# Down product of a seven-product feed-forward layer: the last gated pair stays on the chip and is used third, the residual is added in the middle visits, weights are loaded through GpSimd's queue

## The chip, the cores and the metric

The kernel runs on one core of a Trainium2 chip. The metric is the device time of one launch in microseconds (us). The engines are called by the profile's names: PE is TensorE (PEld its weight loads), DVE is VectorE, ACT is ScalarE, POOL is GpSimd, SP is SyncE, whose queue issues most DMAs. A "q" behind a name (SPq, POOLq) is that engine's sequencer, which works off its instructions strictly in order.

## The reference, cut to what matters

Two layers; each ends with a feed-forward block. Model width is 1024, there are 1024 tokens, and the hidden width is 2816.

```python
def swiglu(h, w_gate, w_up, w_down):
    return (jax.nn.silu(h @ w_gate) * (h @ w_up)) @ w_down

for layer in range(2):
    x = x + mixer(rms_norm(x, ...))
    x = x + memory_cross_attention(rms_norm(x, ...), m, ...)
    x = x + swiglu(rms_norm(x, g_ffn[layer]), w_gate[layer], w_up[layer], w_down[layer])
```

Everything is float32. The change touches only the last product of `swiglu`, and the addition to x.

## The kernel before, in words

Activations lie transposed: 128 features on the partitions, 1024 tokens along the free axis. A *pair* is two such chunks of 128 features, so a 256 x 1024 block, taken as 2 x 2 sub-blocks of 128 x 512. Every block product is formed from seven products of sums of sub-blocks instead of eight (`seven`, L1815). Each operand is cut into a high and a low half that PE multiplies in its rounded float32 format, so one product is three matmuls of 128x512 (`mm`, L441). Making an operand is one ACT copy (high) and one DVE subtraction (low, L454), beside the sums.

Two arenas in on-chip memory hold all data: R (35 x 1024 columns, operands that PE reads) and F (16 x 1024 columns, plain float32; its part "a" is the first 8 x 1024, part "b" the other 8 x 1024). A planner in Python (`run`, L468) walks a list of tasks, one task for each of the seven products, allots space, and makes operands `la` columns ahead of their first use; `raws` bounds how many weight blocks are loaded ahead, `f_reserve` is the part of F that such loads must leave free. The framework's scheduler then orders each engine's instructions by the planner's priorities; each engine and each DMA queue runs its list in order.

The feed-forward block (`ffn`, L1894) runs in two stages. *Gate and up*: for j = 0 to 10, a unit of `w_gate` and one of `w_up` (256 columns, `Unit`, L202) are multiplied with the four pairs of the input, `gated` applies silu, `upped` multiplies the two. `store` (L1926) turns the resulting pair j into its seven operands with four POOL subtractions (L1933), seven ACT copies (L1937) and seven DVE subtractions (L454, through `low`), each in a slot of R, and writes them to device memory `pq` through SP's queue (L1941, seven DMAs for a pair). *Down*: 14 visits (`VISITS`, L32) each take one pair of output chunks (mp = 0 to 3), a stretch lo to hi of the eleven stored pairs, and the block of `w_down` that belongs to them; each of the four output pairs is visited three or four times. The stored pairs come back through SP's queue (`Stored.make`, L361, two DMAs for each operand, 14 for a pair), the weights too (L223). Results are added from PE's accumulator onto x by DVE (`onto_x`, L1876, L1883). `x_back` (L2044, L2047) loads x, which already holds everything but this block's result, into part "a" before the visits: two chunks at j = 9, six at the start of down.

In the first visits everything comes together: the operands of pairs 0 and 1 are loaded into slots of R that the last up unit (j = 10) gives back, pair 10 is still being split and stored, and the weights of the first visits come in.

## Time and profile before

| | |
|---|---|
| median of 3 runs | 2439.45 us (2435.73 to 2440.53) |
| the profiled execution's own time | 2443.61 us |
| its span, first to last instruction | 2441.5 us |
| PE busy | 2356.0 us (96%) |
| DVE busy | 1714.9 us (70%) |
| ACT busy | 1008.5 us (41%) |
| POOL busy | 712.3 us (29%) |
| mean granted TensorE clock | 0.986 of full speed |
| DMA | 350.25 MB, 143 GB/s over the span |

The down stage of layer 0 runs from about 1114 to 1320 us of the span, that of layer 1 from about 2200 to 2430 us. Busy PE is 96% of the span, so what can be won is the rest, and what a lower clock takes from the busy time. It is read stage by stage: a table by windows shows where PE is not busy, the timeline of each engine shows what it waits for there.

### The profile page before, as it was taken

How to read it: one execution, taken by the hardware profiler on the slowest of the kernel's cores; microseconds unless marked ns; L12 is line 12 of the kernel's file. 1: busy time of each engine (PE TensorE's matmuls, PEld its weight loads, DVE VectorE, ACT ScalarE, POOL GpSimd, SP SyncE). 2: the span in 40 equal slices, each digit the busy share in tenths (PEclk: the TensorE clock that was granted, in tenths of full speed). 3: DMA queues.
4: the chain of work that ended last, by engine and by line, in shares of the span. 5: the costliest groups of instructions: out<-in, count | busy, mean ns of one | idle time of the engine just before them, and what ended most of it. 6: DMA issues, size and time to landing. Idle time of an engine off the chain costs nothing.

```text
span 2441.5 us, 31142 instructions
## 1 busy us (share of the span) xinstructions
PE 2356.0 (96%) x11358; PEld 1984.2 (81%) x11358; DVE 1714.9 (70%) x2521; ACT 1008.5 (41%) x1826; POOL 712.3 (29%) x707
## 2 busy tenths in 40 slices
PE   7999999999999999997999999999999999998999
PEld 7999889888878778776888788888878888876887
DVE  5456467864888788878667653355888989887765
ACT  5345366745444444443223311145544444443221
POOL 6542233343433333331001310043433334331000
PEclk9999999999999999999999999999999999999999
DMA  7336334430224344449863221021224434459773
GB/s 229 117 132 208 96 99 136 128 115 27 95 89 153 121 154 150 172 168 340 275 215 117 61 78 52 26 66 48 104 73 143 157 136 165 158 173 382 238 246 95
DMA packets 251649, 350.25 MB, mean 143 GB/s; under 512 B 13376, under 2 KB 151704, under 8 KB 251496
## 3 DMA queue, kind: packets, MB, share of 16 engines
q1 hardware_dynamic: 247664, 335.46, 41.9%
q0 software_dynamic: 3648, 12.75, 1.4%
q8 instruction: 89, 1.46, 0.2%
q14 instruction: 64, 0.52, 0.1%
q10 hardware_dynamic: 184, 0.05, 0.0%
HBM read 233.78 MB, written 114.43 MB: 143 GB/s over the span
## 4 chain that ended last, share of the span: by engine, by line
PE 70%; DVE 14%; DMA 8%; issue 4%; ACT 2%; POOL 1%; SPq 0%; DVEq 0%; ACTq 0%; POOLq 0%
PE psum_t L442 67%; DVE arena_r L454 7%; DMA pq<-arena_r 2%; DMA arena_f<-w_gate 2%; DVE arena_f L233 1%; DVE arena_f L1852 1%; DMA arena_f<-w_up 1%; PE psum_t L1323 1%; DMA arena_f<-w_down 1%; DMA arena_r<-pq 1%; DVE arena_f L1911 1%; ACT arena_r L242 1%; DVE arena_f L1883 1%; DMA arena_f<-e_w_in 1%; PE psum_t L1646 1%
## 5 line engine op out<-in xcount | busy, mean ns | idle before, releaser
L442 PE MATMUL psum_t<-arena_r 128*128 128x512 f32 (+4 forms) x10304 | 2270.7, 379 | 67.0 <-DVE arena_r L454 18.3
L442 PEld LDWEIGHTS psum_t<-arena_r 128*128 128x128 f32 (+1 forms) x10304 | 1860.7, 190 | 423.9 <-DVE arena_r L454 29.8
L454 DVE TENSOR_TENSOR arena_r<-arena_f,arena_r 128x512 fp32r<-128x512 f32 (+4 forms) x803 | 672.7, 858 | 181.8 <-ACT arena_r L242 49.0
L242 ACT CAST arena_r<-arena_f 128x512 fp32r<-128x512 f32 (+2 forms) x504 | 284.6, 583 | 472.2 <-PE psum_t L442 291.9
L1904 POOL TENSOR_TENSOR arena_f<-arena_f 128x512 f32<-128x512 f32 x88 | 160.4, 1828 | 488.5 <-ACT arena_f L1903 488.5
L233 DVE TENSOR_TENSOR arena_f<-arena_f 128x512 f32<-128x512 f32 (+2 forms) x288 | 208.6, 728 | 91.8 <-DMA arena_f<-w_down 50.9
L1883 DVE TENSOR_TENSOR arena_f<-psum_t,arena_f 128x512 f32<-128x512 f32 x224 | 148.4, 685 | 61.0 <-PE psum_t L442 60.4
L1933 POOL TENSOR_TENSOR arena_f<-arena_f 128x512 f32<-128x512 f32 x88 | 144.5, 1661 | 88.4 <-DVE arena_f L1911 64.7
L1937 ACT CAST arena_r<-arena_f 128x512 fp32r<-128x512 f32 x154 | 95.5, 621 | 175.2 <-DVE arena_f L1911 64.2
L1852 DVE TENSOR_TENSOR arena_f<-psum_t,arena_f 128x512 f32<-128x512 f32 x176 | 119.4, 683 | 36.5 <-PE psum_t L442 19.6
L686 POOL TENSOR_TENSOR arena_f<-arena_f 128x1024 f32<-128x1024 f32 x21 | 60.6, 2885 | 274.8 <-ACT arena_f L682 176.5
L572 ACT CAST arena_r<-arena_f 128x1024 fp32r<-128x1024 f32 (+1 forms) x57 | 59.0, 1042 | 109.3 <-PE psum_t L442 94.5
L454 DVE TENSOR_TENSOR arena_r<-psum_t,arena_r 128x512 fp32r<-128x512 f32 (+3 forms) x124 | 84.5, 703 | 21.7 <-ACT arena_r L1650 7.9
L1903 ACT ACTIVATE arena_f<-arena_f 128x512 f32<-128x512 f32 x88 | 55.4, 632 | 74.6 <-DVE arena_f L1902 74.4
L1313 POOL TENSOR_SCALAR arena_f<-arena_f,small 128x640 f32<-128x640 f32 (+6 forms) x64 | 48.4, 765 | 109.4 <-DVE small L1312 105.3
L1911 DVE TENSOR_TENSOR arena_f<-arena_f 128x512 f32<-128x512 f32 x88 | 71.8, 816 | 5.8 <-POOL arena_f L1904 2.4
L1902 DVE TENSOR_TENSOR arena_f<-arena_f 128x512 f32<-128x512 f32 x88 | 65.7, 747 | 4.3 <-ACT arena_f L714 4.1
L465 POOL TENSOR_TENSOR small<-small,mhalf 128x4 f32<-128x4 f32 (+1 forms) x64 | 63.2, 988 | 5.2
L1308 ACT ACTIVATE arena_f<-psum_t,small 128x640 f32<-128x640 f32 (+6 forms) x64 | 47.5, 744 | 22.4 <-DVE small L1306 19.5
L1306 DVE TENSOR_REDUCE small<-psum_t 128x1 f32<-128x640 f32 (+5 forms) x64 | 47.2, 750 | 7.5 <-PE psum_t L442 7.1
L2112 POOL TENSOR_TENSOR arena_f<-arena_f 128x1024 f32<-128x1024 f32 x4 | 10.4, 2608 | 139.3 <-DVE arena_f L2064 134.5
L1636 POOL TENSOR_SCALAR arena_f<-arena_f,small 128x256 f32<-128x256 f32 x64 | 30.4, 495 | 68.3 <-DVE small L1633 58.9
(187 smaller groups left out, 1442.1 us busy)
## 6 DMA issues: line engine op xcount, KB each, us to landing
pq<-arena_r SPq DMA_DIRECT2D x154, 512.0 KB
arena_r<-pq SPq DMA_DIRECT2D x308, 256.0 KB
arena_f<-w_gate SPq DMA_DIRECT2D x22, 1024.0 KB
arena_f<-w_up SPq DMA_DIRECT2D x22, 1024.0 KB
arena_f<-xs SPq DMA_DIRECT2D x32, 512.0 KB
arena_r<-qk SPq DMA_DIRECT2D x48, 256.0 KB
arena_f<-w_down SPq DMA_DIRECT2D x12, 1024.0 KB
qk<-arena_r POOLq DMA_DIRECT2D x16, 512.0 KB, 4.2
```

The source lines that it names most:

```text
L233: getattr(T.nc, self.adds).tensor_tensor(out=out, in0=a, in1=b, op=what)
L242: T.nc.scalar.copy(out=hv, in_=src)
L442: self.nc.tensor.matmul(out=out, lhsT=lhsT, rhs=rhs, start=start, stop=stop, skip_group_check=again)
L454: getattr(self.nc, eng).tensor_tensor(out=out, in0=src, in1=high, op=ALU.subtract)
L465: self.nc.gpsimd.tensor_tensor(out=out, in0=in_, in1=self.mhalf[:, 0:in_.shape[-1]], op=ALU.pow)
L1852: nc.vector.tensor_tensor(out=o, in0=bank[q].ap, in1=o if other is None else other, op=ALU.add)
L1883: nc.vector.tensor_tensor(out=o, in0=bank[q].ap, in1=o, op=ALU.add)
L1902: nc.vector.tensor_tensor(out=q, in0=q, in1=r, op=ALU.mult)
L1904: nc.gpsimd.tensor_tensor(out=q, in0=q, in1=r, op=ALU.mult)
L1911: nc.vector.tensor_tensor(out=c[j].ap[:, o], in0=c[j].ap[:, o], in1=s.ap[:, o], op=ALU.mult)
L1933: nc.gpsimd.tensor_tensor(out=out, in0=a, in1=b, op=ALU.subtract)
L1937: nc.scalar.copy(out=t.ap[:, 0:512], in_=src)
```

## The change

- `Unit` takes its rows as a list of stretches, and the name of the engine whose queue loads it. Down units are loaded through POOL's queue (gate and up units stay on SP's). The first two down units may lie in either part of F ("ba"), before in "b" alone.
- The last pair (j = 10) is not given to `store`. `FreshPair` keeps its two F chunks, makes the same four POOL subtractions (the last two in place, as `store` did) and the same seven ACT copies and DVE subtractions, but straight into the R slots from which PE reads them. Nothing of that pair goes to `pq` or comes back.
- The order of the pairs in down is 0, 1, 10, 2, 3, ..., 9, so the kept pair is the third.
- `x_back` is gone. The first four visits, one for each output pair, start their chunks of x afresh (`collected`: three ACT copies and four DVE additions a visit, instead of eight DVE additions). In visits 5 to 8 (counted from 0) `add_x` loads the two chunks of the old x through POOL's queue into part "b" and adds them with one DVE addition of 128x1024 each.
- `raws` is 4 for the start of down, then 2; `f_reserve` is 2048 in down instead of 0.

```diff
-        T.nc.sync.dma_start(
-            out=raw.ap.rearrange("p (k c) -> p k c", k=2 * n),
-            in_=self.src[self.r0:self.r0 + 2 * n * P, self.c0:self.c0 + 256].rearrange("(k p) c -> p k c", p=P))
+        k = 0
+        for r0, m in self.rows:
+            getattr(T.nc, self.queue).dma_start(
+                out=raw.ap[:, k * 512:(k + m) * 512].rearrange("p (k c) -> p k c", k=2 * m),
+                in_=self.src[r0:r0 + 2 * m * P, self.c0:self.c0 + 256].rearrange("(k p) c -> p k c", p=P))
+            k += m
...
+class Fresh:
...
+    def make(self, T, must):
+        pair = T.room_for(512, "ab", must)
+        if pair is None:
+            return False
+        self.h, self.l = pair
+        src = self.pair.block(T, self.i)
+        T.nc.scalar.copy(out=self.h.ap, in_=src)
+        T.low(self.l.ap, src, self.h.f)
+        self.pair.used(self.i)
+        return True
...
+class FreshPair:
...
+        def op(out, a, b):
+            T.nc.gpsimd.tensor_tensor(out=out, in0=a, in1=b, op=ALU.subtract)
+        if i == 0:
+            self.t1, self.t2 = T.F.get(512, "ba"), T.F.get(512, "ba")
+            op(self.t1.ap, b12, b11)
+            op(self.t2.ap, b22, self.t1.ap)
+        if i == 1:
+            op(b12, b22, b12)
+        if i == 3:
+            op(b21, b21, self.t2.ap)
+        return (b11, b21, self.t2.ap, self.t1.ap, b12, b21, b22)[i]
...
-                    store(f // 2, c)
+                    if f + 2 == NF:
+                        fresh.c = c
+                    else:
+                        store(f // 2, c)
...
-            if j == 9:
-                self.add(lambda: self.x_back(0, 2))
...
-            self.x_back(2, KD)
-            self.reserve, self.la, self.f_reserve = 0, 4096, 0
+            self.x = [None] * KD
+            self.reserve, self.la, self.f_reserve, self.raws = 0, 4096, 2048, 4
...
+        which = [0, 1, NF // 2 - 1] + list(range(2, NF // 2 - 1))
+        home = "b" if finish else "ba"
+        ps = [StoredPair(self.pq[layer, j], home if n >= 9 else "ab") for n, j in enumerate(which)]
+        ps[2] = fresh
...
+        def add_x(mp):
+            got = []
+            for k in (2 * mp, 2 * mp + 1):
+                t = self.F.get(S, "b")
+                nc.gpsimd.dma_start(out=t.ap, in_=self.xs[k * P:(k + 1) * P, :])
+                got.append((k, t))
+
+            def fn():
+                for k, t in got:
+                    nc.vector.tensor_tensor(out=self.x[k].ap, in0=self.x[k].ap, in1=t.ap, op=ALU.add)
+                    t.free()
+            self.defer(fn, 6)
...
+            u = Unit(wd, rows, hi - lo + 1, mp * 256, "ba" if n < 2 else "b", "b" if finish and left <= 4 else "ba", queue="gpsimd")
+            if n == 1:
+                self.add(lambda: setattr(self, "raws", 2))
+            if 5 <= n < 9:
+                self.add(lambda mp=mp: add_x(mp))
...
+            self.tasks += self.seven(u, ps[lo:hi + 1],
+                                     self.collected(opened_x(mp), "ab") if n < 4 else
+                                     self.onto_x(2 * mp, quarter_of(mp, left <= 2) if left <= 4 else None))
```

## Rows read from the trace of the kernel before

**Rows 1.** Table by windows of both starts of down; columns in its first line.

```profile
core 0: us, PE busy (x) PEld busy (x) DVE busy (x) ACT busy (x) POOL busy (x), PEclk, DMA share, GB/s
1080.00:1114.00 34.00, 29.62 (x126) 22.74 (x124) 26.99 (x32) 13.28 (x23) 13.88 (x8) 1.00 0.70 237
1114.00:1170.00 56.00, 43.71 (x173) 34.34 (x174) 41.36 (x78) 17.00 (x37) 5.96 (x4) 0.91 0.99 347
1170.00:1340.00 170.00, 169.62 (x748) 140.02 (x747) 116.08 (x192) 46.23 (x79) 5.77 (x3) 1.00 0.61 202
2170.00:2200.00 30.00, 23.98 (x96) 19.04 (x95) 22.87 (x27) 11.50 (x20) 9.45 (x6) 0.89 0.65 215
2200.00:2260.00 60.00, 51.80 (x214) 41.20 (x214) 44.60 (x85) 18.64 (x40) 6.07 (x4) 0.94 1.03 375
```

**Rows 2.** Timeline, PE, layer 0: start, length, line, operation, count, [idle before <-releaser].

```profile
1134.27 4.38 PE L442 MATMUL psum_t<-arena_r 128*128 128x512 f32 x18 [1.53 <-DMA arena_r<-pq]
1147.00 6.64 PE L442 MATMUL psum_t<-arena_r 128*128 128x512 f32 x21 [8.35 <-DVE arena_f L233]
1155.77 19.60 PE L442 MATMUL psum_t<-arena_r 128*128 128x512 f32 x78 [2.13 <-ACT arena_r L242]
```

**Rows 3.** Timeline, PE, layer 1.

```profile
2230.78 10.59 PE L442 MATMUL psum_t<-arena_r 128*128 128x512 f32 x35 [5.78 <-ACT arena_r L242]
2242.96 2.35 PE L442 MATMUL psum_t<-arena_r 128*128 128x512 f32 x9 [1.58 <-DMA arena_r<-pq]
```

**Rows 4.** Timeline, ACT, layer 0, just before the long wait of PE.

```profile
1138.90 0.62 ACT L1937 CAST arena_r<-arena_f 128x512 fp32r<-128x512 f32 x1 [2.90 <-DMA pq<-arena_r]
1144.42 0.62 ACT L1937 CAST arena_r<-arena_f 128x512 fp32r<-128x512 f32 x1 [4.91 <-DMA pq<-arena_r]
1146.44 2.17 ACT L242 CAST arena_r<-arena_f 128x384 fp32r<-128x384 f32 x5 [1.40 <-DMA arena_f<-w_down]
```

**Rows 5.** Timeline, SP's queue, layer 0: DMAs as they were issued.

```profile
1113.83 18.79 SPq L361 DMA_DIRECT2D arena_r<-pq  x22
...
1134.29 0.69 SPq L223 DMA_DIRECT2D arena_f<-w_down  x1
...
1146.24 0.46 SPq L223 DMA_DIRECT2D arena_f<-w_down  x1
```

**Rows 6.** Waits of SP's queue, 1100 to 1340: total us, times, longest.

```profile
SPq L361 <- PE psum_t L442: 101.7, 62, 9.7
```

**Rows 7.** Timeline, POOL, layer 0: one group after another, nothing left out between.

```profile
1132.70 6.03 POOL L1933 TENSOR_TENSOR arena_f<-arena_f 128x512 f32<-128x512 f32 x4 [22.83 <-DVE arena_f L1911]
1315.19 2.40 POOL L686 TENSOR_TENSOR arena_f<-arena_f 128x1024 f32<-128x1024 f32 x1 [176.46 <-ACT arena_f L682]
```

**Rows 8.** Instructions that touch xs: ns min/median/max, first and last start.

```profile
L2047 SPq DMA_DIRECT2D arena_f<-xs x16: 320/378/736, 982.5 to 2198.5; - x16
L788 POOL DMA_DIRECT2D xs<-arena_f x8: 929/968/1011, 12.9 to 63.5; - x8
...
DMA to landing us min/median/max: 3.9/5.3/7.0
```

**Rows 9.** Page, costliest groups: busy us, mean ns | idle before, releaser.

```profile
L1883 DVE TENSOR_TENSOR arena_f<-psum_t,arena_f 128x512 f32<-128x512 f32 x224 | 148.4, 685 | 61.0 <-PE psum_t L442 60.4
L1933 POOL TENSOR_TENSOR arena_f<-arena_f 128x512 f32<-128x512 f32 x88 | 144.5, 1661 | 88.4 <-DVE arena_f L1911 64.7
L1937 ACT CAST arena_r<-arena_f 128x512 fp32r<-128x512 f32 x154 | 95.5, 621 | 175.2 <-DVE arena_f L1911 64.2
```

**Rows 10.** Page, DMA issues: count and KB each.

```profile
pq<-arena_r SPq DMA_DIRECT2D x154, 512.0 KB
arena_r<-pq SPq DMA_DIRECT2D x308, 256.0 KB
```

**Rows 11.** Timeline, DVE, layer 0: the last quarter of pair 10; then the split's release.

```profile
1131.94 0.68 DVE L1911 TENSOR_TENSOR arena_f<-arena_f 128x512 f32<-128x512 f32 x1
...
1142.41 1.15 DVE L233 TENSOR_TENSOR arena_f<-arena_f 128x384 f32<-128x384 f32 x2 [1.11 <-DMA arena_f<-w_down]
```

More of the change, by code (lines that the diff above doesn't have):

```diff
@@ L202, with __init__ @@
 class Unit:
-    def __init__(self, src, r0, n, c0, where="b", home="ba", adds="vector"):
-        self.src, self.r0, self.n, self.c0 = src, r0, n, c0
+    def __init__(self, src, rows, n, c0, where="b", home="ba", adds="vector", queue="sync"):
+        self.src, self.rows, self.n, self.c0, self.queue = src, rows, n, c0, queue
         self.where, self.home, self.adds = where, home, adds
@@ L371, in __init__, with ready, fetch, done @@
         self.ops = [Stored(src[i], home) for i in range(7)]
+class Fresh:
+    cols = 512
+    heavy = False
+    def __init__(self, pair, i):
+        self.pair, self.i = pair, i
+        self.left = 0
+    def ready(self):
+        return self.pair.c is not None
+    def fetch(self, T, must):
+        return True
[8 more added lines that the diff above has]
+        self.pair.used(self.i)
+        return True
+    def done(self):
+        self.h.free()
+        self.l.free()
+class FreshPair:
+    def __init__(self):
+        self.c = None
+        self.ops = [Fresh(self, i) for i in range(7)]
+    def block(self, T, i):
+        b11, b12 = self.c[0].ap[:, 0:512], self.c[0].ap[:, 512:1024]
+        b21, b22 = self.c[1].ap[:, 0:512], self.c[1].ap[:, 512:1024]
+        def op(out, a, b):
[9 more added lines that the diff above has]
+        return (b11, b21, self.t2.ap, self.t1.ap, b12, b21, b22)[i]
+    def used(self, i):
+        if i == 3:
+            self.t1.free()
+        if i == 4:
+            self.c[0].free()
+            self.t2.free()
+        if i == 6:
+            self.c[1].free()
 class Task:
@@ L1897, in ffn @@
         st = {}
+        fresh = FreshPair()
         def gated(j, half, c):
@@ L1994, in ffn @@
                 self.tasks += ut[2:]
-            if j == 9:
-                self.add(lambda: self.x_back(0, 2))
         def down_start():
             self.rbc.free()
-            self.x_back(2, KD)
-            self.reserve, self.la, self.f_reserve = 0, 4096, 0
+            self.x = [None] * KD
+            self.reserve, self.la, self.f_reserve, self.raws = 0, 4096, 2048, 4
         self.add(down_start)
-        ps = [StoredPair(self.pq[layer, j], "ba" if j >= 9 else "ab") for j in range(NF // 2)]
-        if finish:
-            for p in ps[9:]:
-                for o in p.ops:
-                    o.home = "b"
+        which = [0, 1, NF // 2 - 1] + list(range(2, NF // 2 - 1))
+        home = "b" if finish else "ba"
+        ps = [StoredPair(self.pq[layer, j], home if n >= 9 else "ab") for n, j in enumerate(which)]
+        ps[2] = fresh
         waiting = []
@@ L2025, in quarter_of, with opened_x, fn @@
             return fn
+        def opened_x(mp):
+            def fn(j, half, c):
+                self.x[2 * mp + j] = c[j]
+            return fn
+        def add_x(mp):
[9 more added lines that the diff above has]
+            self.defer(fn, 6)
         def open_now():
@@ L2036, in ffn @@
             left = len(VISITS) - n
-            u = Unit(wd, lo * 256, hi - lo + 1, mp * 256, "b", "b" if finish and left <= 4 else "ba")
+            rows = []
+            for j in which[lo:hi + 1]:
+                if rows and rows[-1][0] + rows[-1][1] * 256 == j * 256:
+                    rows[-1] = rows[-1][0], rows[-1][1] + 1
+                else:
+                    rows.append((j * 256, 1))
+            u = Unit(wd, rows, hi - lo + 1, mp * 256, "ba" if n < 2 else "b", "b" if finish and left <= 4 else "ba", queue="gpsimd")
[3 more added lines that the diff above has]
+                self.add(lambda mp=mp: add_x(mp))
             if left == 2 and finish:
@@ L2041, in ffn @@
                 self.add(down_end)
-            self.tasks += self.seven(u, ps[lo:hi + 1], self.onto_x(2 * mp, quarter_of(mp, left <= 2) if left <= 4 else None))
-    def x_back(self, lo, hi):
-        for k in range(lo, hi):
-            self.x[k] = self.F.get(S, "a")
-            self.nc.sync.dma_start(out=self.x[k].ap, in_=self.xs[k * P:(k + 1) * P, :])
+            self.tasks += self.seven(u, ps[lo:hi + 1],
+                                     self.collected(opened_x(mp), "ab") if n < 4 else
+                                     self.onto_x(2 * mp, quarter_of(mp, left <= 2) if left <= 4 else None))
     def odd(self):
```

4 lines of the change are left out of this document (2 added, 2 removed).

## The prediction
> **What bounds the kernel now.** PE is busy for nearly all of the span, so I looked first for the stretches in which it isn't. The table by windows cuts each start of down in two [rows 1]. From 1170 on PE is full (169.62 of 170 us, clock 1.00): nothing can be won there, and work may be added beside it as long as it does not stop PE. The loss sits in the start of down: in layer 0, 1114 to 1170, PE is busy 43.71 of 56 us at a clock of 0.91; in layer 1, 2200 to 2260, 51.80 of 60 us at 0.94. A busy microsecond at 0.91 does 0.91 of a full one's work, so the lost time is 12.29 + 43.71 x 0.09 = 16.2 us in layer 0 and 8.20 + 51.80 x 0.06 = 11.3 us in layer 1, 27.5 us together. That is the most that this change can win where it works. The windows just before (1080 to 1114, 2170 to 2200) lose 4.4 us and 6.0 + 24.0 x 0.11 = 8.6 us more, but they belong to unit j = 10 of gate and up, whose loads the change leaves on SP's queue and in part "b".
>
> Next, what PE waited for. In layer 0 there are three gaps: 1.53 us for an operand from pq, 8.35 us before a product whose weights had not been made, 2.13 us for a weight cast [rows 2]; in layer 1, 5.78 us for a weight cast and 1.58 us for pq [rows 3]. The 8.35 us are read on ACT and on SP. ACT, in order, stood 2.90 and 4.91 us in two of pair 10's split copies, each waiting until an earlier *store* of pair 10 had left its R slot; only then, at 1146.44, came the weight casts [rows 4]. DVE had begun on those weights at 1142.41 [rows 11], so they had landed; ACT was late because of the stores. The weights themselves were issued late too: behind 22 pq loads, at 1134.29, and the third load after four more stores, at 1146.24 [rows 5]. The pq loads wait for PE to free R slots (101.7 us in layer 0) [rows 6], and whatever stands behind them in that queue waits too. All through this window the DMA engines are full (share 0.99, 347 GB/s; layer 1: 1.03, 375 GB/s) [rows 1].
>
> **The change part by part.** *Pair 10 kept.* This takes seven stores of 512 KB and 14 loads of 256 KB out of each layer [rows 10], 3.67 MB each way. The stores and the loads of the third pair, which no longer come from pq, both leave the full window: 7.34 MB, at 347 GB/s 21 us of transfers in a window that loses 16.2 us. It also takes the two ACT waits of 2.90 and 4.91 us away. The split is not saved: four POOL subtractions, seven ACT copies, seven DVE subtractions stay, 4 x 1.661, 7 x 0.621 and 7 x about 0.69 us (an estimate from the equally large additions of L1883) [rows 9]. They are now needed by PE. The last quarter of pair 10 is multiplied at 1131.94 [rows 11]; operands 0 and 1 are plain sub-blocks and need only a copy and a subtraction, 1.3 us each; operand 2 needs two POOL subtractions first, 1131.94 + 0.68 + 2 x 1.66 + 1.3 = about 1137.3. Without its gap for pq, PE would end visits 0 and 1 at 1138.65 - 1.53 = about 1137; visit 2's products (nine matmuls each, at 170/748 us about 2 us) [rows 1] then want operand 2 at about 1141. That is 4 us of slack, with DVE crowded (41 of 56 us busy). I therefore keep a remainder of 2.5 us of waiting for each layer; its bounds are 0 (the operands are early) and 8 us (POOL's or ACT's list holds other waits ahead of the split, as ACT's did for 2.90 + 4.91 us).
>
> *Weights through POOL's queue.* 14 loads a layer, or 18 with those whose rows are in two stretches. POOL's own DMA issues took 0.97 us each [rows 8], so 18 us a layer; POOL is idle from the end of its split at 1138.7 until 1315 [rows 7], so this lies beside PE and costs nothing. If POOL were not idle it would cost up to 1 us a visit. Landing from POOL's queue was 5.3 us for 512 KB, for writes while the DMA engines had room [rows 8]; a 1 MB load in the full window should need about 8 us, as the one issued at 1134.29 and first used at 1142.41 did [rows 5, 11]. Loaded ahead (four blocks instead of two), they land during visits 0 and 1. What moves behind a waiting POOL instruction: pair 10's four subtractions, if a later block's load waits there for its buffer; that is in the 8 us bound. SP's queue loses these waits for its own followers, the pq loads.
>
> What the issuing queue is worth is where rule and row differ. The row shows a weight load held back on SP until 1134.29 by loads that wait for PE, with the DMA engines full. The Trainium skill, "DMA: Bandwidth & Descriptors", section "Issuing engines are not separate DMA queues", says that all issuing engines share the same 16 DMA engines and that a second one saves only the sequencer's issue time, usually little. By that rule the move brings nothing, and the sum would be that of rival 2 below; by the row the sequencer's wait is itself the delay, and the sum is the one here.
>
> *The residual.* `x_back` takes eight loads of 0.52 MB away, but not from the full window: in layer 0 they start at 982.5 and seven are out before 1057, one is at 1109.9 [rows 8]. So this removes only 0.52 MB, 1.5 us of transfer, from the window. The first four visits save 16 DVE additions of 0.685 us [rows 9], 11 us, and gain 12 ACT copies of about 0.6 us; the middle gains eight DVE additions over 1024 columns, at twice 0.685 us 11 us in all, and 4.2 MB of loads. There DVE is busy 116 of 170 us and the DMA engines 0.61 [rows 1], so it is hidden; with DVE full it would cost up to 11 us a layer. I take 0.
>
> Sum: 27.5 - 2 x 2.5 = 22.5 us. The profiled execution took 2443.6 us, 4.2 us over the median of the runs; 22.5 us off gives 2421.1 for such an execution, and 2439.45 - 22.5 = **2417 us** as median.
>
> **The rivals.** *1, more is won.* With x not in the way and SP's list shorter, part of the 4.4 + 8.6 us lost in unit j = 10 goes as well, and the remainder is zero: 2439.45 - 27.5 - 6.5 (half of 13.0) = 2405. Against it: nothing in the change moves that unit's loads. *2, the weights come no earlier.* They share full DMA engines with the pq loads: if the block for visit 2 is still landing 8.1 us after about 1133, at 1141, PE stops 4 us there and again about 2 us for the next block, so 6.5 us a layer more: 2417 + 13 = 2430. It decides if the DMA share stays near 1.0 up to visit 2. Against it: 21 us of transfers are gone. *3, the middle visits starve (slower).* In visits 5 to 8 two x chunks take 2048 of part "b"'s 8192 columns, a full weight block 2560, and 2048 must stay free, so no second block is fetched while the chunks are there. If a block's load then starts only when the x addition has been made, six products into a visit of about 19 us (84 matmuls), 8.1 us of landing meet about 3 us of cover: 5 us a visit, 4 visits, 2 layers, 40 us: 2417 + 40 = 2457, slower. It decides once a load has less than a visit of lead; with a block's place free one visit early, as the planner's order has it by my count (the block before gives its place back at the visit's third product), it costs nothing. *4, the wait is only exchanged.* PE meets pair 10's split instead of its stores: POOL's list has a weight load waiting for a buffer, ACT waits in the split copy, the weight casts wait behind. At 8 us a layer for that and 6.5 us for late weights, 27.5 - 29 = -1.5: 2441, no change.
>
> **How the numbers follow.** Forecast 0.60; rival 1 0.08; rival 2 0.10; rival 3 0.13; rival 4 0.09. About 5 us (0.2%) is what a measurement of this kernel can tell from no change. Faster: 0.60 + 0.08 + 0.10 = 0.78; same 0.09; slower 0.13. The forecast's own range is 2412 (remainder 0) to 2428 (remainder 8 us a layer). With rivals 1 and 2, 2404 to 2436 holds about 0.8.
>
> **What would show it.** Right: in the windows after the last up product PE is busy without a gap over 3 us and the clock stays 1.00; no L1941 store and no ACT wait for one there; weight loads on POOL's queue issued before visit 1 ends; DMA share below 0.9 by visit 2; in the middle visits PE stays at 10.0 of 10 us. Wrong: PE or ACT waiting for the split's POOL subtractions (rival 4), for w_down in visits 2 and 3 (rival 2) or in visits 6 to 9 (rival 3). The gaps of unit j = 10 should still be there; if they are not, rival 1.

## The result and the profile after

The changed kernel takes 2425.53 us (median of 6 runs, 2421.68 to 2429.26) against 2439.55 us for the kernel before, run beside it on the same chip: 0.9938 of the time, 95% interval 0.9925 to 0.995. The gain is 14.0 us where 22.5 were forecast; 2425.5 lies in the range, 8.5 us above its point. The profiled execution took 2428.93 us with a span of 2427.2, 14.3 us less span than before.

First the place where the gain was expected. The profile after, table by windows, columns as in [rows 1]: the stretch of the last gate and up unit, the two starts of down, and the middle visits of each layer.

```profile
1080.00:1114.00 34.00, 27.26 (x106) 20.77 (x105) 24.93 (x37) 13.87 (x26) 15.61 (x11) 0.90 0.69 233
1114.00:1170.00 56.00, 53.85 (x237) 43.93 (x236) 42.19 (x75) 24.59 (x50) 12.99 (x14) 1.00 0.73 255
2200.00:2260.00 60.00, 60.00 (x267) 49.69 (x266) 45.61 (x79) 26.18 (x50) 12.74 (x14) 1.00 0.80 278
1180.00:1300.00 120.00, 120.00 (x531) 99.36 (x530) 82.12 (x132) 24.93 (x43) 9.17 (x13) 1.00 0.76 259
2270.00:2380.00 110.00, 110.00 (x489) 91.10 (x488) 79.48 (x132) 25.39 (x47) 8.26 (x12) 1.00 0.77 265
```

The starts of down lose 2.15 us (layer 0) and nothing (layer 1), where [rows 1] lost 16.2 and 11.3. The DMA share fell from 0.99 and 1.03 to 0.73 and 0.80, the granted clock is 1.00, and PE is full in the middle visits. But the first line, the window before down in layer 0, has PE busy for 27.26 of 34 us at a clock of 0.90, where [rows 1] had 29.6 at 1.00: here something got worse. PE's timeline after, in both layers (start, us, count, and in brackets the idle time before and what ended it):

```profile
1097.39 5.49 PE L510 MATMUL psum_t<-arena_r 128*128 128x512 f32 x12 [4.37 <-DVE arena_f L1920]
1104.04 38.58 PE L510 MATMUL psum_t<-arena_r 128*128 128x512 f32 x168 [1.16 <-ACT arena_r L245]
1143.20 1.20 PE L510 MATMUL psum_t<-arena_r 128*128 128x512 f32 x4 [0.58 <-ACT arena_r L245]
1145.96 201.88 PE L510 MATMUL psum_t<-arena_r 128*128 128x512 f32 x886 [1.57 <-DVE arena_r L522]
...
2179.07 5.49 PE L510 MATMUL psum_t<-arena_r 128*128 128x512 f32 x12 [4.31 <-DVE arena_f L1920]
2185.47 187.26 PE L510 MATMUL psum_t<-arena_r 128*128 128x512 f32 x824 [0.92 <-ACT arena_r L245]
```

Compare [rows 2] and [rows 3]: the gaps of 8.35 and 5.78 us are gone, and PE runs 201.88 and 187.26 us at a stretch. The page shows what left (pair 10's 14 stores and 28 loads, [rows 10]) and what POOL now issues:

```profile
L225 POOL DMA_DIRECT2D arena_f<-w_down x38 | 30.4, 800 | 181.3 <-DVE arena_r L522 101.8
...
pq<-arena_r SPq DMA_DIRECT2D x140, 512.0 KB
arena_r<-pq SPq DMA_DIRECT2D x280, 256.0 KB
```

**Where the time went.** Four instructions of PE that occur in both kernels cut the span: the four matmuls that spread the scales, in layer 0, in the odd layer's start and in layer 1, and the first of the last transposes. PE's timeline of before, then of after:

```profile
700.51 1.88 PE L442 MATMUL psum_t<-arena_f,ones 128*128 128x512 f32 x4
1381.07 1.88 PE L442 MATMUL psum_t<-arena_f,ones 128*128 128x512 f32 x4
1796.12 1.88 PE L442 MATMUL psum_t<-arena_f,ones 128*128 128x512 f32 x4
2434.99 1.60 PE L2191 MATMUL psum_t<-ident,arena_f 128*128 128x128 f32 x12
```

```profile
700.65 1.88 PE L510 MATMUL psum_t<-arena_f,ones 128*128 128x512 f32 x4
1370.72 1.88 PE L510 MATMUL psum_t<-arena_f,ones 128*128 128x512 f32 x4
1786.11 1.88 PE L510 MATMUL psum_t<-arena_f,ones 128*128 128x512 f32 x4
2420.25 1.60 PE L2285 MATMUL psum_t<-ident,arena_f 128*128 128x128 f32 x12
```

Layer 0's block went from 680.6 to 670.1 us (1381.07 - 700.51, and so on), layer 1's from 638.9 to 634.1. Each block holds gate and up first and down after it. I split it where the last up unit (j = 10) starts: 1099.27 before and 1104.04 after in layer 0; in layer 1 2185.47 after, and before 2188.5, since 12 matmuls are still missing there at 2183.89 and run about 4.6 us, most of it at a clock of 0.50. Up to its cut each layer has run the same number of matmuls before and after, 1661 in layer 0 and 1654 in layer 1. The last up unit itself, 84 matmuls or about 19 us, so stands on the side of down. (The expectations below count layer 1 of the kernel before from 2183.89: 387.8 and 251.1 us.)

| us | gate and up to the last up unit, before | after | from there on (down), before | after |
|---|---|---|---|---|
| layer 0 | 398.8 | 403.4 (+4.6) | 281.8 | 266.7 (-15.1) |
| layer 1 | 392.4 | 399.4 (+7.0) | 246.5 | 234.8 (-11.7) |

So down gained 26.8 us, more than the sum of the prediction had it; gate and up, which the prediction left at nothing, lost 11.6; start and odd layer lost 0.5. That makes 14.7 us, the distance of the last rows above. These are single executions; the odd layer's start, whose work no run changes, takes 414.4 to 415.8 us in all profiles but one (417.2), so a block's difference of about 1 us says nothing.

**The loss in layer 0** lies in its last unit. DVE after, and the load on POOL that belongs to it:

```profile
1089.93 0.88 POOL L225 DMA_DIRECT2D arena_f<-w_down  x1 [1.14 <-DVE arena_r L522]
...
1096.31 0.43 DVE L236 TENSOR_TENSOR arena_f<-arena_f 128x256 f32<-128x256 f32 x1 [4.56 <-DMA arena_f<-w_down]
1096.66 0.68 DVE L1920 TENSOR_TENSOR arena_f<-psum_t,arena_f 128x512 f32<-128x512 f32 x1
```

DVE, in order, stood 4.56 us before the addition that makes a *down* weight (L236), whose data were still on their way, and the collecting addition of the gate unit (L1920), for which PE waited 4.37 us, stood behind it. PE then ran its next 12 matmuls in 5.49 us, where the same 12 took 3.01 us in the kernel before. Windows of the clock (after in layer 0; then before in layer 1, where the same happens):

```profile
1097.30:1102.90 5.60, 5.49 (x12) 3.80 (x12) 2.27 (x5) 1.26 (x2) 2.95 (x2) 0.50 0.93 336
```

```profile
2183.80:2188.00 4.20, 4.11 (x10) 3.23 (x11) 4.20 (x8) 2.96 (x6) 0.34 (x1) 0.50 0.52 178
```

In both the granted clock after the gap is 0.50, the lower of its two levels. So the gap of 4.4 us takes 6.9 us of PE in layer 0 (4.37 + 5.49 - 3.01). But it is not what sets the time. The last up unit cannot start before its own weights are cast; the load of these weights on SP and the first cast on ACT, before and then after:

```profile
1091.67 0.46 SPq L223 DMA_DIRECT2D arena_f<-w_up  x1
1098.60 0.62 ACT L242 CAST arena_r<-arena_f 128x512 fp32r<-128x512 f32 x1 [4.28 <-DMA arena_f<-w_up]
```

```profile
1092.60 1.98 SPq L225 DMA_DIRECT2D arena_f<-w_up  x1
1103.37 2.18 ACT L245 CAST arena_r<-arena_f 128x512 fp32r<-128x512 f32 x4 [3.10 <-DMA arena_f<-w_up]
```

The weights came 6.9 us after the load was issued in the kernel before, and 10.8 us after it in the changed one. PE was through with the 12 slow matmuls at 1102.88 and still waited 1.16 us for this cast. The slower landing (3.8 us) and a load issued 0.8 us later, both counted from the spread, make the 4.6 us; the stall of DVE and the slow clock lie inside that wait. Ahead of w_up two down loads had just gone out on POOL (1089.93 and 1091.45). Over the runs below, the time from the issue of this load to its first use in layer 0 is 6.9 and 7.1 us with no down load just ahead (before, `pair_only`), 7.9 and 9.3 with one (`pair_x`, `late`), and 8.6 to 10.8 with two (`sync`, `rbc_place`, after). That the down loads delay w_up is read from this; no run moves them alone.

In layer 1 the kernel before had its own gap there (4.80 us, for w_up too), so this unit costs about the same before and after.

**The loss in layer 1** lies earlier, in a stretch that the diff doesn't touch. Windows of gate and up, before and then after:

```profile
700.00:1060.00 360.00, 349.05 (x1511) 283.07 (x1511) 303.46 (x403) 161.38 (x283) 129.66 (x73) 1.00 0.43 148
1800.00:2150.00 350.00, 345.70 (x1509) 283.25 (x1508) 304.35 (x403) 160.75 (x282) 127.82 (x74) 1.00 0.44 153
```

```profile
700.00:1060.00 360.00, 349.87 (x1514) 283.89 (x1513) 303.36 (x404) 161.23 (x283) 131.34 (x73) 1.00 0.40 139
1800.00:2150.00 350.00, 340.51 (x1483) 276.85 (x1482) 299.43 (x396) 154.49 (x273) 129.74 (x74) 1.00 0.40 140
```

Layer 0 is as it was (three matmuls more). Layer 1 does 1483 matmuls instead of 1509 by 2150 us: 26 x 0.23 = 6.0 us behind, with a full clock and a DMA share that is *lower* than before. (The stage starts 10 us earlier after; windows at the same distance from the spread give 1483 and 1508.) What PE waits for in the stretch from 1800 to 2150, before and then after (total us, times, longest):

```profile
PE psum_t L442 <- DVE arena_r L454: 2.7, 2, 1.9
PE psum_t L510 <- DVE arena_r L522: 6.9, 9, 1.7
```

Both lines are the subtraction that makes the low half of an operand: DVE comes late with it nine times instead of twice.

### The profile page after: what moved, and what is told of

The parts are those of the page before. It is cut to its first block, busy times and chain, and to the rows that moved or that the text cites. A ratio compares the mean times of both kernels' runs of the same rounds, so it can differ in the third digit from the quotient of the medians.

```text
span 2427.2 us, 31163 instructions
## 1 busy us (share of the span) xinstructions
PE 2352.7 (97%) x11358; PEld 1981.8 (82%) x11358; DVE 1708.3 (70%) x2505; ACT 1019.5 (42%) x1850; POOL 752.7 (31%) x761
## 4 chain that ended last, share of the span: by engine, by line
PE 72%; DVE 12%; DMA 7%; issue 4%; POOL 2%; ACT 2%; SPq 0%; DVEq 0%; ACTq 0%; POOLq 0%
PE psum_t L510 69%; DVE arena_r L522 6%; DMA arena_f<-w_gate 2%; DMA arena_f<-w_up 2%; DMA pq<-arena_r 2%; DVE arena_f L236 1%; DVE arena_f L1920 1%; POOL arena_f L2005 1%; PE psum_t L1391 1%; DVE arena_f L1980 1%; ACT arena_r L245 1%; DMA arena_f<-e_w_in 1%; PE psum_t L1714 1%; DVE arena_f L1764 1%; DVE arena_r L742 0%
## 5 line engine op out<-in xcount | busy, mean ns | idle before, releaser
L522 DVE TENSOR_TENSOR arena_r<-arena_f,arena_r 128x512 fp32r<-128x512 f32 (+4 forms) x803 | 662.8, 847 | 175.0 <-PE psum_t L510 47.2
L1973 POOL TENSOR_TENSOR arena_f<-arena_f 128x512 f32<-128x512 f32 x88 | 164.3, 1873 | 475.2 <-ACT arena_f L1972 475.2
L236 DVE TENSOR_TENSOR arena_f<-arena_f 128x512 f32<-128x512 f32 (+2 forms) x288 | 207.7, 724 | 92.1 <-DMA arena_f<-w_down 53.2
L1920 DVE TENSOR_TENSOR arena_f<-psum_t,arena_f 128x512 f32<-128x512 f32 x208 | 141.0, 683 | 52.8 <-PE psum_t L510 33.7
L2009 ACT CAST arena_r<-arena_f 128x512 fp32r<-128x512 f32 x140 | 86.8, 621 | 161.0 <-DVE arena_f L1980 62.6
L2005 POOL TENSOR_TENSOR arena_f<-arena_f 128x512 f32<-128x512 f32 x80 | 132.2, 1672 | 46.2 <-DVE arena_f L1980 44.6
L1951 DVE TENSOR_TENSOR arena_f<-psum_t,arena_f 128x512 f32<-128x512 f32 x160 | 105.5, 683 | 41.8 <-PE psum_t L510 41.5
L225 POOL DMA_DIRECT2D arena_f<-w_down x38 | 30.4, 800 | 181.3 <-DVE arena_r L522 101.8
L1930 ACT COPY arena_f<-psum_t 128x512 f32<-128x512 f32 x52 | 30.3, 584 | 55.0 <-PE psum_t L510 47.2
```

Source lines behind the costliest of these rows:

```text
L236: getattr(T.nc, self.adds).tensor_tensor(out=out, in0=a, in1=b, op=what)
L522: getattr(self.nc, eng).tensor_tensor(out=out, in0=src, in1=high, op=ALU.subtract)
L1920: nc.vector.tensor_tensor(out=o, in0=bank[q].ap, in1=o if other is None else other, op=ALU.add)
L1951: nc.vector.tensor_tensor(out=o, in0=bank[q].ap, in1=o, op=ALU.add)
L1973: nc.gpsimd.tensor_tensor(out=q, in0=q, in1=r, op=ALU.mult)
L2005: nc.gpsimd.tensor_tensor(out=out, in0=a, in1=b, op=ALU.subtract)
```

## The experiments

Four theories for the 11.6 us and one for the gain. A: the first two down units are loaded so early, on POOL's queue, that their weights stand ahead of gate and up's work. B: the tile of the spread scales (`rbc`) has moved to another place. C: x has moved: its eight tiles are now opened by down's first four visits and no longer loaded by `x_back`, so the allocator puts them elsewhere, and the places that x holds decide where, and when, layer 1's other tiles find room. D: the kept pair alone makes the gain; the residual and the queue add nothing to it. Against D stands that the weights' queue does the work, as the prediction's row argued. Block lengths (spread to spread, layer 0, and spread to last transposes, layer 1) stand beside each ratio; before has 680.6 and 638.9, after 670.1 and 634.1.

### A: no early loads

The first two units of down may not be fetched before down starts, unless they must.

```
+        if not must and self.opens and not T.down_open:
+            return False
...
+            self.down_open = True
...
+            u.opens = n < 2
```

> The changed kernel, with one thing held back: the first two down units are not loaded before the last up task is planned (they come with the others at the start of down). Theory A, their early load through POOL's queue delays unit j = 10: DVE's list holds their first addition ahead of the eviction of a gate product, and the w_up load behind them lands late. Then the waits of PE for L1920 (4.37 us in layer 0, 4.31 us in layer 1) go, the time from the spread of the scales to the first product of the last up unit falls from 403.4 to about 399 us in layer 0 and from 399.4 to about 396 us in layer 1, and the run takes about 2417 us if down starts as before. Rival: the wait is only moved, and PE waits as long for w_down at the start of visit 0; then the run stays at 2425 us.

Measured: 0.9954 (0.9939 to 0.9969), blocks 668.6 and 639.8: not faster than after. In the trace one of the two down loads still goes out early (on POOL at 1086.84, ahead of w_up's on SP at 1088.51 in layer 0), so the edit holds back the second alone. PE's timeline, layer 0, then ACT's (lines are three higher than in after):

```profile
1090.37 3.01 PE L513 MATMUL psum_t<-arena_r 128*128 128x512 f32 x12 [1.40 <-DVE arena_f L1923]
1098.49 18.21 PE L513 MATMUL psum_t<-arena_r 128*128 128x512 f32 x72 [5.10 <-ACT arena_r L248]
...
1097.82 2.18 ACT L248 CAST arena_r<-arena_f 128x512 fp32r<-128x512 f32 x4 [2.56 <-DMA arena_f<-w_up]
```

The 4.37 us before the collecting addition are 1.40 again and these 12 matmuls run in 3.01 us, so the stall in layer 0 did come from the early loads. But PE then waits 5.10 us, and not for a down weight: ACT's cast is one of w_up's weights, which came 9.3 us after their issue. The time from the spread to the last up unit is 399.9 us in layer 0, as theory A had it (403.4 after), and 400.2 in layer 1, where 396 was expected (399.4 after). The slow stretch now lies behind the cut (clock 0.70 from 1098.4 to 1104, 0.55 from 2182.1 to 2188), and down takes 268.7 and 239.6 us, 2.0 and 4.8 more than after. So A is right about the cause in layer 0 and, in this form, wrong as a remedy; the rival, a wait for w_down at visit 0, is not what the trace shows either.

### The restriction on the last unit

Another reading of the same gap: the loads of unit j = 10 come too late, because they may use part "b" alone. By the code, that restriction kept part "a" free for `x_back`, which no longer exists.

```
-            g = Unit(wg, [(0, 4)], 4, j * 256, "b" if j == 10 else "ba")
-            u = Unit(wu, [(0, 4)], 4, j * 256, "b" if j == 10 else "ba")
+            g = Unit(wg, [(0, 4)], 4, j * 256, "ba")
+            u = Unit(wu, [(0, 4)], 4, j * 256, "ba")
```

> The changed kernel, with the gate and up units of j = 10 allowed in both parts of F, as the other units are. Theory A': the stalls of unit j = 10 (4.4 and 8.6 us before the change, about as much after it) come from that restriction, since the planner can then load them only when they are due; without it the spread-to-last-up time falls to about 393 us in layer 0 and 390 us in layer 1, and the run takes about 2409 us. Rival: w_up of j = 10 is late because SP's queue stands in the stores of pair 9; then the w_up load is issued as late as now and nothing changes (2425 us).

Measured: 0.9883 (0.9863 to 0.9902), blocks 669.1 and 624.1: 10 us of layer 1, 1 us of layer 0. The median is 2415 us where 2409 was expected. The load of w_up for j = 10 goes out at 1043.24 in layer 0, 49 us earlier than in after, and up to the cut the layers take 394.5 and 387.1 us (expected about 393 and 390). PE's timeline at that unit and, in layer 0, at the start of down:

```profile
1097.27 1.43 PE L510 MATMUL psum_t<-arena_r 128*128 128x512 f32 x5 [0.71 <-ACT arena_r L245]
...
1137.45 3.67 PE L510 MATMUL psum_t<-arena_r 128*128 128x512 f32 x13 [1.31 <-ACT arena_r L245]
1141.49 22.75 PE L510 MATMUL psum_t<-arena_r 128*128 128x512 f32 x99 [0.38 <-DVE arena_r L522]
1167.06 13.32 PE L510 MATMUL psum_t<-arena_r 128*128 128x512 f32 x45 [2.81 <-DVE arena_f L1920]
...
2174.18 1.45 PE L510 MATMUL psum_t<-arena_r 128*128 128x512 f32 x5 [0.65 <-ACT arena_r L245]
```

The wait before that unit is under 1 us in both layers, where after waited 4.37 and 4.31 and ran the next 12 matmuls slowly. In layer 1 that is kept to the end; in layer 0 the start of down waits 1.31 + 0.38 + 2.81 = 4.5 us instead of 2.15, the clock is 0.56 for 7 us behind the last of these gaps, and down takes 274.6 us instead of 266.7: most of the gain is gone.

### B: the place of the spread scales

`rbc` gets fixed slots, 112 in layer 0 and 32 in layer 1, instead of what the allocator gives.

```
-        self.rbc = self.F.get(S, "ba")
+        self.rbc = self.F.get(S, "ba") if at is None else self.F.take(at * 64, S)
```

> The changed kernel, with the row of scales (rbc, 1024 columns that live through gate and up) put at another place of part a: 112 in layer 0 (there 64), 32 in layer 1 (80; before the change it lay at 32). Theory B: layer 1's gate and up got 10 us longer (378.7 to 388.7 us up to the end of the last full run of gate products) because rbc cuts part a in another place and weights come later. Then layer 1 goes back to about 379 us, layer 0 changes by some us either way, and the run takes about 2415 us or less. Rival: it is the order that the scheduler found, whatever the place; then layer 1 stays within 2 us of 388.7.

Measured: 0.9933 (0.9919 to 0.9948), blocks 670.8 and 634.9; gate and up of layer 1 takes 400.1 us, after 399.4. B falls.

### The weights on SP's queue again

```
-            u = Unit(wd, rows, ..., queue="gpsimd")
+            u = Unit(wd, rows, ..., queue="sync")
```

> The changed kernel, with the down weights on SP's queue again (all else as changed). If the queue is what counts, the weights of visits 2 and 3 come late behind pq loads and PE waits 4 to 8 us a layer at the start of down: about 2437 us. If the removed stores and loads are what counts, down starts without a gap over 3 us all the same and, since w_up of j = 10 is no longer overtaken by w_down on another queue, the run takes 2420 to 2426 us.

Measured: 0.9930 (0.9915 to 0.9945), blocks 668.0 and 635.0: the same time as after. With SP's queue down takes 265.0 and 236.3 us by the split above, 266.7 and 234.8 with POOL's. The longest wait of PE from 1100 on, in layer 0, and the run of matmuls behind it:

```profile
1102.10 98.24 PE L510 MATMUL psum_t<-arena_r 128*128 128x512 f32 x426 [3.13 <-ACT arena_r L245]
```

This cast, too, is one of w_up's weights (issued at 1092.74, first used at 1101.38); behind it PE runs through, in layer 1 as well (60.00 of 60 us busy from 2200 on). So the queue is worth nothing here. The row that spoke for it, a weight load held until 1134.29 behind pq loads [rows 5], was true of a queue that had seven stores and 14 loads more to carry in front of a full DMA; with these gone SP issues the first four down loads between 1087.9 and 1121.0, where the kernel before issued its third and fourth at 1134.29 and 1136.71. By the Trainium skill, "DMA: Bandwidth & Descriptors", section "Issuing engines are not separate DMA queues", a second issuing engine saves only the sequencer's issue time; the measured 0.9930 against 0.9938 agrees.

### D: the kept pair alone

The kernel before with `FreshPair` and its third place in the order, and nothing else: the residual comes back by `x_back`, the weights stay on SP's queue with two blocks.

```
-                    store(f // 2, c)
+                    if f + 2 == NF:
+                        fresh.c = c
+                    else:
+                        store(f // 2, c)
...
+        which = [0, 1, NF // 2 - 1] + list(range(2, NF // 2 - 1))
...
+        ps[2] = fresh
```

> The kernel before, with the kept pair alone: pair 10 is split in place and used third; x is loaded back early and the down weights come through SP's queue, as before. Theory D, the stores and loads that are gone are what makes down start without gaps: the time from the first product of the last up unit to layer 1's spread of scales at the start of the next block falls from 281.8 to 266 to 270 us in layer 0, and from 251.1 to 235 to 240 us to the end in layer 1; the run has a ratio of about 0.990. Rival: the weights on SP's queue stand behind pq loads and PE waits for them at visits 2 and 3, 4 to 8 us a layer: 272 to 276 us and 241 to 246 us, ratio 0.994 to 0.996.

Measured: 0.9889 (0.9864 to 0.9913), median 2413.0 us, blocks 663.9 and 627.3: faster than the whole change. Windows at the starts of down:

```profile
1114.00:1170.00 56.00, 56.00 (x248) 46.36 (x247) 51.71 (x92) 18.79 (x39) 5.86 (x4) 1.00 0.82 280
...
2200.00:2260.00 60.00, 60.00 (x267) 49.67 (x266) 54.08 (x90) 18.52 (x34) 5.11 (x4) 1.00 0.78 261
```

No gap and a full clock in both, with DVE busy for 51.71 of 56 us (the residual's additions are still here). Gate and up stays as it was: 399.6 us in layer 0, and 392.9 in layer 1, counted as above. By the expectation's count down takes 264.3 us in layer 0, below the 266 to 270 that theory D gave, and 238.7 in layer 1, within its 235 to 240.

### The whole change without the kept pair

```
-                    if f + 2 == NF:
-                        fresh.c = c
-                    else:
-                        store(f // 2, c)
+                    store(f // 2, c)
...
-        which = [0, 1, NF // 2 - 1] + list(range(2, NF // 2 - 1))
+        which = list(range(NF // 2))
```

> The changed kernel, with pair 10 stored and loaded again as before, in the order 0 to 10; the residual and the weights' queue as changed. Theory D: the gaps at the start of down come back, 278 to 283 us in layer 0 and 246 to 252 us in layer 1 from the first product of the last up unit on, and with the longer gate and up of layer 1 the run is as slow as the kernel before or slower, ratio 0.999 to 1.005. Rival: the weights loaded ahead and the later residual do it; then 267 to 272 and 235 to 240 us, ratio 0.994 to 0.996.

Measured: 1.0043 (1.0028 to 1.0058), blocks 680.8 and 650.7: slower than before. The windows, and PE's line of layer 1:

```profile
1114.00:1170.00 56.00, 48.49 (x199) 38.94 (x198) 37.29 (x63) 20.70 (x42) 9.23 (x9) 0.94 1.00 354
2200.00:2260.00 60.00, 49.60 (x207) 40.21 (x206) 38.92 (x72) 22.33 (x46) 12.41 (x9) 0.91 0.94 325
```

```profile
2244.87 55.43 PE L510 MATMUL psum_t<-arena_r 128*128 128x512 f32 x235 [10.39 <-ACT arena_r L245]
```

The full DMA (share 1.00 and 0.94) and the gaps are back, with the weights on POOL's queue: PE waits 10.39 us for a cast of them. By the expectation's count down takes 276.7 us in layer 0 and 249.7 in layer 1, where the kernel before has 281.8 and 251.1. D holds from both sides: the pair alone gives as much in down as the whole change and more, the other two parts without it give a few microseconds in layer 0, next to nothing in layer 1, and lose them elsewhere.

### C: x in the places that it had before

The x tiles that layer 0's first four visits start go to the slots that x had before.

```
-                st["c"].append(self.F.get(S, where))
+                st["c"].append(self.F.get(S, where) if at is None else self.F.take(at[len(st["c"])] * 64, S))
...
+   at = {1: (112, 80), 2: (32, 48), 3: (96, 64), 0: (0, 16)}[mp] if layer == 0 else None
```

> The changed kernel, with the eight chunks of x that layer 0's first four visits start put in those slots of part a in which x lay before the change. Nothing else is changed, and the planner's order is the same. Theory C: layer 1's gate and up got longer (387.8 to 399.4 us from the spread of the scales to the first product of the last up unit) because other slots give the scheduler other conflicts and it finds another order of the weight loads and DVE work. Then layer 1 goes back to 388 to 391 us there, and the run takes about 10 us less than the changed kernel, a ratio to the kernel before of about 0.990. Rival: the length comes from something that the change does in down (its own loads, POOL's queue); then it stays at 398 to 400 us and the ratio at 0.994.

Measured: 0.9917 (0.9894 to 0.994), blocks 667.5 and 630.1. Gate and up of layer 1 takes 395.4 us; its window:

```profile
1800.00:2150.00 350.00, 344.97 (x1503) 282.23 (x1502) 305.04 (x400) 156.58 (x276) 125.17 (x74) 1.00 0.40 140
```

1503 matmuls instead of 1483: of the 7.0 us, 4.0 come back by places alone, by one profile of each kernel. Theory C expected more (388 to 391 by its count, where 395.4 was found), and the interval of the ratio holds both its 0.990 and the rival's 0.994. So C is borne out for about half of the loss; about 3 us stay.

### The residual alone, on top of the pair

`pair_only` with x started afresh in the first visits and `add_x` in the middle ones instead of `x_back`, and with it `f_reserve` 2048 in down as in the change (`pair_only` has 0); the weights stay on SP's queue.

```
-        self.x_back(2, KD)
+        self.x = [None] * KD
...
+            if 5 <= n < 9:
+                self.add(lambda mp=mp: add_x(mp))
```

> The kept pair and the later residual, with the down weights on SP's queue, in part b and two ahead as before. Theory E, the later residual brings nothing where down starts, and by giving x other slots it lengthens layer 1's gate and up: against the kept pair alone (663.9 and 627.3 us for the two layers) layer 0 stays within 3 us and layer 1 takes 632 to 636 us, ratio 0.992 to 0.994. Rival: the loss against the kept pair alone comes from the early weight loads, which this kernel lacks; then layer 1 takes 626 to 629 us and the ratio is 0.989.

Measured: 0.9947 (0.993 to 0.9964), median 2425.44, blocks 665.3 and 635.3: 1.4 and 8.0 us longer than `pair_only`, and in layer 1 the window of gate and up again:

```profile
1800.00:2150.00 350.00, 341.21 (x1481) 277.70 (x1480) 296.05 (x394) 155.90 (x276) 130.09 (x73) 1.00 0.40 141
```

1481 matmuls instead of `pair_only`'s 1511. The later residual loses in the stage *after* it what the prediction valued at nothing, and wins nothing at the start of down, where `pair_only` has no gap left. Of the 8.0 us 6.4 lie before the cut of layer 1. What `f_reserve` does in this was not tried alone.

### Places alone, in the kernel before

The work stays what it was; only the eight tiles of x that enter layer 0 lie in other slots, and the planner orders the rest around them.

```
-                self.x.append(self.F.take(k * S, S))
+                self.x.append(self.F.take((0, 1, 7, 5, 2, 3, 6, 4)[k] * S, S))
```

> The kernel before, with one thing changed: ahead of layer 0's feed-forward block, the eight chunks of x lie in slots 0, 1, 7, 5, 2, 3, 6, 4 of part a in place of 0 to 7. No work is added or taken away. Theory C, the places alone change the order that the scheduler finds in gate and up: layer 0 (680.6 us from the spread of the scales to the next block's) gets 8 to 16 us shorter, as it did with the j = 10 units freed (669.1 to 653.1 us); layer 1, whose plan then starts from other free slots, may change by up to 10 us the other way. Rival: the 16 us belonged to the changed down stage; then layer 0 stays within 3 us of 680.6.

Measured: 1.0011 (1.0001 to 1.0022); blocks 673.6 and 645.0, so layer 0 gains 7.0 us and layer 1 loses 6.1. Its windows:

```profile
700.00:1060.00 360.00, 355.52 (x1549) 289.15 (x1548) 313.12 (x412) 162.12 (x286) 128.70 (x76) 1.00 0.44 150
1800.00:2150.00 350.00, 339.37 (x1478) 275.85 (x1478) 297.51 (x394) 154.36 (x274) 129.76 (x74) 1.00 0.44 153
```

In layer 0 1549 matmuls instead of 1511, in layer 1 1478 instead of 1509. The 7.0 us are a little under the 8 to 16 of theory C and well over the 3 of its rival. This is the cleanest evidence that the places of x alone move a layer by 6 to 7 us in either direction.

### The parts put together

After with the restriction on j = 10 lifted and both sets of slots (`both_free`), and the pair alone with the restriction lifted and layer 0's slots (`pair_free`).

> The changed kernel with unit j = 10 allowed in both parts of F, x after layer 0 in the slots of before, and x in layer 0 too in other slots (0, 1, 7, 5, 2, 3, 6, 4 in place of 0 to 7). Theory C: layer 0's gate and up get shorter too, by up to 10 us, if these slots give an order as good as layer 1's; with the j = 10 stalls gone the run has a ratio of 0.983 to 0.988. Rival: layer 0's order does not depend on the slots, and the run is that of the kernel with unit j = 10 freed alone, ratio 0.988.

> The kept pair alone, with the gate and up units of j = 10 in both parts of F and x in layer 0 in the slots 0, 1, 7, 5, 2, 3, 6, 4. If the three gains add up: layer 0 about 663.9 - 1 - 16 = 647 us, layer 1 about 627.3 less up to 8 us for the j = 10 stalls, 619 to 628 us; ratio 0.978 to 0.984, the fastest of all. Rival: without the residual's place in part a freed, the units of j = 10 find no room earlier and layer 0 stays above 655 us; ratio 0.985 to 0.989.

Measured: `both_free` 0.9844 (0.9824 to 0.9865), median 2402.49, blocks 653.1 and 628.3; `pair_free` 0.9855 (0.984 to 0.9869), median 2404.77, blocks 654.3 and 627.5. The intervals overlap; worked out from the ratios both beat before by 35 to 38 us and after by 20 to 23. In `both_free` layer 0 gains 16.0 us on `ba10` (669.1 to 653.1) by slots alone; in its window

```profile
700.00:1060.00 360.00, 354.50 (x1546) 288.69 (x1545) 317.24 (x417) 163.46 (x288) 131.64 (x77) 1.00 0.42 145
```

PE does 1546 matmuls instead of the 1509 of `ba10`. Layer 1, on the other hand, is 4.2 us longer than in `ba10` (628.3 against 624.1): the gains of single places don't add up. `both_free` came out as expected; `pair_free` did not (647 us for layer 0 and a ratio of at most 0.984 were expected), its ratio is the one that its rival gave. That each change of places alters the next stage's is the likely reason, and argued.

## Why the prediction came out as it did

**The mechanism: right.** The kept pair took the stores and loads out of a full DMA, the gaps at the starts of down went, and the clock came back. Down gained 26.8 us; the sum had 22.5 of at most 27.5. The term for what remains was about right in layer 0 and too large in layer 1: 2.5 us a layer assumed, 2.15 and 0 found. Its reason was pair 10's split, and POOL's part of that was timed well: operand 2 was put at 1137.3, and the stage runs 4.8 us later (1104.04 - 1099.27), which makes it 1142.1. POOL, then ACT, after:

```profile
1137.28 0.76 POOL L225 DMA_DIRECT2D arena_f<-w_down  x1 [13.99 <-DVE arena_f L1920]
1138.06 4.37 POOL L421 TENSOR_TENSOR arena_f<-arena_f 128x512 f32<-128x512 f32 x3
...
1142.64 1.34 ACT L245 CAST arena_r<-arena_f 128x384 fp32r<-128x384 f32 x3 [2.62 <-DMA arena_f<-w_down]
```

Two of the three subtractions end at about 1141.0 (1138.06 + 2 x 4.37 / 3), and 1.3 us more for copy and subtraction would give 1142.3. But PE did not wait for the split. ACT stood 2.62 us for the weights of visit 2, whose larger load POOL had issued only at 1137.28, after a wait of 13.99 us, and made the split's next copy behind their casts, at 1143.88. PE's gaps of 0.58 and 1.57 us there are for a cast and a subtraction of these weights. So the 2.15 us are a small piece of rival 2, and that they are near the 2.5 of the sum is luck.

One reading of the rows was wrong, without a consequence for the sum. The prediction has the weights landed at 1142.41 in the kernel before, and ACT late because of pair 10's stores. The load that landed then, issued at 1134.29, is another block; the cast that released PE at 1146.44 waited for the load issued at 1136.71. [rows 4] says so: ACT was free at 1145.04 (1144.42 + 0.62) and stood another 1.40 us for w_down. The stores delayed ACT, but a load that took 9.7 us beside full DMA engines ended the 8.35 us.

**The number: partly luck.** 2425.5 us lies within 2412 to 2428, but the width of that range stood for waits of up to 8 us a layer on the split. With the remainder that was found its terms give 2439.45 - 27.5 + 2.15 = about 2414 us. What brought the time back towards the slow end is a loss that the sum had at nothing.

**The step that failed: what the change leaves alone costs nothing.** "They belong to unit j = 10 of gate and up, whose loads the change leaves" is true of the diff and not of the time, and "I take 0" for the residual was bounded by the work that it adds (DVE and DMA in the middle visits, both hidden, as said: PE is full there). What it missed is 11.6 us, worked out above as +4.6 and +7.0:

- 4.6 in layer 0: the change left that unit's load on SP's queue, but its own down loads went out just ahead of it, and the weights came 10.8 us after their issue instead of 6.9. The stall of DVE that the same loads caused lies inside that wait. `late` takes away the stall and one of the two loads, and the last up unit starts 3.5 us earlier (399.9 against 403.4); over both layers `late` loses 6.8 us again in down.
- 7.0 in layer 1: x's tiles lie elsewhere after the later residual. `pair_x` makes 8.0 us of loss out of the later residual and its reserve, `x_slots` gives 4.0 back by places alone, and `before_slots` moves 6 to 7 us by places in the kernel before.

**Weights through POOL's queue.** The prediction valued it by the row that showed loads held behind SP's queue, and made "the weights come no earlier" a rival of 2430 us. As a mechanism for this kernel that rival is wrong (no DMA share near 1.0, no wait of PE over 1.6 us at the starts of down), but so was the row's reading: `sync` and `stored` together show that the delay came from pair 10's stores and loads, not from the queue. The costs were right: 38 issues (36 counted) of 0.80 us instead of 0.97, beside PE; the landing of a 1 MB block 7.6 us instead of about 8, though the load that the 8 us were read from was one of 768 KB (three pairs, 128x384).

**The other rivals.** Rival 1 (j = 10 gains too) didn't happen in the change, but the gain that it named is there: lifting the restriction on that unit shortens the two blocks by 11 us. The prediction read that the unit was in part "b" and didn't ask whether it had to stay there. Rival 3 (the middle visits starve) is excluded: PE is busy 120.00 of 120 and 110.00 of 110 us. Rival 4 (the wait is only exchanged) was right about an exchange and wrong about its place: not pair 10's split but the weights of the unit before it, in one layer, at a third of the price (4.6 us against 14.5).

**Open.** About 3 us of layer 1's 7.0 are not explained by the slots of layer 0 that were tried, nor by `rbc`, nor by the early loads. And why a place changes the time is argued, not shown: another place lets a buffer be had earlier or later, and the planner then orders loads and splits around it differently. The waits that change are those for DVE's subtractions, but no run set the order by itself, and none tells it from a rival that was not tried, that the engines are served at another speed in other slots.

## What to carry to other kernels

When a change moves or frees buffers, compare the stages that the diff does not touch, matmul for matmul: here they took back 11.6 of 26.8 us. Change one part at a time: the one part that carried the gain was faster alone (0.9889) than with the two that came with it (0.9938). And when a step is removed, remove what was there for its sake: the restriction on unit j = 10 kept room for `x_back`, and lifting it won 11 us after that was gone. (`pair_free` runs with `x_back` and without the restriction, so it was not needed even there; what it costs in the kernel before, no run tells.)

## What was not expected of the hardware

A gap of PE of 4.3 to 4.8 us is followed by a stretch at a granted clock of 0.50 in three places (after in both layers, before in layer 1), and one of 2.81 us in `ba10` by 7 us at 0.56: the next 12 matmuls took 5.49 us in after instead of 3.01, half as much again as the gap itself. Whether the kernel pays for it depends on what PE would have waited for anyway: in layer 0 of after it lay inside the wait for w_up. And eight buffers of SBUF in another order, with the same work to do, move one layer by 7.0 us and the other by 6.1 the other way; whether through the chip or through the planner's order, no run tells.
